# FFN down projection: sixteen of 22 inner tiles as seven block products, sums and splits through PSUM, parts split amid the up projection

## The chip, the core and the metric

The kernel runs on one core of a Trainium2 chip. The metric is the device time of one execution, in microseconds (us). The core has five engines with queues of their own, which meet only at semaphores: TensorE (PE in the profile, PEld its weight loads), VectorE (DVE), ScalarE (ACT), GpSimd (POOL) and SyncE (SP), whose queue issues the DMA transfers. Operands lie in SBUF, matmul results in PSUM, and the inputs, outputs and scratch arrays in HBM.

## The reference

One decoder layer on 1024 tokens of width 1024. The change lies in its last part, a gated MLP with 2816 = 22 x 128 inner channels:

```
h = rms_norm(x, pre_ffn_norm[l])
u = causal_dwconv(h @ ffn_w_up[l], ffn_conv_w[l], ffn_conv_b[l])
gate, val = jnp.split(u, 2, axis=-1)
f = (jax.nn.gelu(gate, approximate=True) * val) @ ffn_w_down[l]
x = x + rms_norm(f, post_ffn_norm[l])
```

All of it is float32. The kernel works on transposed data: 128 channels on the partitions, 512 tokens (a half, h = 0 or 1) along a row.

## The kernel before, in words

**Products.** A float32 operand is split in two numbers of a shorter format: `hi` is the rounded value (a ScalarE copy), `lo` the rest (a subtraction). A product is three matmuls, hi x hi, hi x lo and lo x hi, summed in a PSUM bank. All matmuls are issued in line 203. The tail's pool `psd` has five banks (`dense`), `psn` three more.

**Up projection.** For inner tiles f = 4 to 21, `up_pair` makes gate and value tile in one go, by seven block products in place of eight (Winograd's form of Strassen's scheme): the weights and the activations are cut in 2 x 2 blocks, four weight sums are made on GpSimd and split (`weights7`), the activations' sums `rhs` were made earlier. Each of the seven products is 12 matmuls. Three banks x, y, z accumulate: x takes products 1, 6, 5 and 3 in turn, y takes 2, z takes 7 and 4. Between two of them ScalarE copies the bank's state to SBUF (`snap`), and what is to be subtracted or added is done by VectorE or GpSimd. A causal convolution (`conv`, lines 301 to 309), the gelu (L1471) and the gating product (L1475) follow, and the gated tile goes to HBM (`m_d`).

**First splits.** In eight of these pairs, `first_split` loads a tile of chunk 0 back, splits it (L1449, L1450) and stores both parts (`mhi_d`, `mlo_d`).

**Down projection.** It runs over chunks of inner tiles, `DOWN`: 4, 4, 4, 4, 2 and at last 4 tiles. For each of eight output tiles j and both halves, `down` makes the products of a chunk in one bank and adds it to the sum `acc[h][j]` (L1584, L1586). `m_split` loads and splits a chunk's tiles, `load_w` (L265 to L268) loads and splits the weights, with GpSimd's subtraction. The last chunk goes in three groups of tokens (`LAST`) with the norm behind each; its weights are split ahead by VectorE (`w_split`). `x1_d`, the residual, comes by two 2 MB transfers.

**Order.** A scheduler places the instructions on each engine's queue by its own estimates; pools with a fixed number of buffers (`hi`, `lo` 16 each, `x` 26, `u0`, `u1` four each) and explicit edges bind it. Each queue then runs strictly in order, so an instruction that waits holds up all behind it on its engine.

Of the kernel before, what the change touches and what calls it, by code (L numbers as in the profile page):

```python
# [1241 lines left out]
def tail_stage(nc, tc, es, env):  # L1242
# [144 lines left out]
    def weights7(src0, src1, n):  # L1387

        raws = []
        for m, src in enumerate((src0, src1)):  # L1390
# [24 lines left out]
        return {1: (whi[:, lo], wlo[:, lo]), 2: (whi[:, up], wlo[:, up]), 3: (h24[:, up], l24[:, up]),  # L1415
                4: (ahi, alo), 5: (h31[:, up], l31[:, up]), 6: (h24[:, lo], l24[:, lo]), 7: (h31[:, lo], l31[:, lo])}

    def product(ps, w, rhs, q, first):
        hi, lo = w[q]
        for k, b in enumerate(rhs[q]):  # L1420
            s = slice(k * 128, (k + 1) * 128)
            for n, (x, y) in enumerate(((hi, b[0]), (hi, b[1]), (lo, b[0]))):
                mm(ps, x[:, s], y, start=first and k == 0 and n == 0, stop=k == len(rhs[q]) - 1 and n == 2,
                   skip_group_check=True)

    def bank():
        return psd.tile([128, 512], F32, name="dense", tag="dense")

    def snap(ps):
        s = up_.tile([128, 512], F32, name="snap", bufs=5)  # L1430
        act(s, ps, AF.Copy)
        return s
# [10 lines left out]

    def first_split(f, h):
        raw = x_t(F32)
        nc.sync.dma_start(raw, m_d[f * 128:(f + 1) * 128, hs(h)])
        yield
        parts = [up_.tile([128, 512], R32, name=f"u{s}") for s in range(2)]
        act(parts[0], raw, AF.Copy)  # L1449
        V.tensor_tensor(parts[1], raw, fl(parts[0]), op=OP.subtract)  # L1450
# [39 lines left out]
    def up_pair(f, rhs, between=None):  # L1490

        st = {}
        w = weights7(A["wup"][2 * f], A["wup"][2 * f + 1], 512)
# [4 lines left out]
        V.tensor_tensor(y, y, s1, op=OP.add)
        conv(2 * f, 0, y, st)
        product(x, w, rhs, 6, False)  # L1500
        s2 = snap(x)
# [8 lines left out]
        V.tensor_tensor(z, z, s2, op=OP.subtract)  # L1510
# [47 lines left out]

    acc = []

    def m_tile(f, h, s):
        t = up_.tile([128, 512], F32, name=f"u{s}")
        nc.sync.dma_start(t, m_d[f * 128:(f + 1) * 128, hs(h)])
        return t

    def m_split(f, h):
        src = m_tile(f, h, f % 2)
        hi, lo = hi_t(), lo_t()
        act(hi, src, AF.Copy)
        V.tensor_tensor(lo, src, fl(hi), op=OP.subtract)  # L1570
        return hi, lo

    def m_chunk(f0, nf):
        return {(f, h): m_split(f, h) for h in range(2) for f in range(f0, f0 + nf)}

    def down(ci, f0, nf, ms, ws=()):
        end = None
        for j in range(8):
            w = ws[j] if j < len(ws) else load_w(A[f"wdn{ci}"][j], nf * 128)
            pss = fm_unit(psd, w, lambda k, h: ms[f0 + k, h], nf)  # L1580
            for h, ps in enumerate(pss):
                a = acc[h][j]
                if ci == 0:
                    act(a, ps, AF.Copy)  # L1584
                else:
                    end = V.tensor_tensor(a, a, ps, op=OP.add)  # L1586
# [18 lines left out]
    tc.keep_in_program_order(nc.scalar.preload_act_table_set(E.TABLE))
    for ci, (f0, nf) in enumerate(DOWN[:last]):
        if ci == 0:
            acc = [[x_t(F32) for _ in range(8)] for _ in range(2)]
        i = down(ci, f0, nf, m_chunk(f0, nf) if ci else ms0, () if ci else ws0)
        if ci == last - 2:  # L1610
            late = i
# [5 lines left out]
    def w_split(j, place):
        ws.append(load_w(A[f"wdn{last}"][j], 512, place, up_.tile([128, 512], F32, name="snap", bufs=5)))

    for k in range(nf):  # L1620
        ms[k][0] = m_split(f0 + k, 0)
    for j in range(4):
        w_split(j, (x_t(), x_t()))
    for k in range(nf):
        ms[k][1] = m_split(f0 + k, 1)
    for j in range(4, 8):
        w_split(j, (hi_t(), lo_t()))
    wx_.close()
    x1p = es.enter_context(tc.tile_pool(name="x1", reuse_waits="tile", bufs=1))
    x1s = [x1p.tile([128, 8, 512], F32, name=f"x1_{h}") for h in range(2)]  # L1630
    with tc.issue_after(late.ins):
        for h in range(2):
# [69 lines left out]
```

## Time and profile before

| | |
|---|---|
| median of 3 runs | 2251.07 us (2251.02 to 2253.52) |
| the profiled execution | 2251.32 us, of which the profile's span is 2249.6 us |
| mean granted TensorE clock | 0.989 |
| DMA traffic over the span | 213.44 MB, mean 95 GB/s |
| up pairs | about 1646 to 1992 us of the span |
| down projection and its norms | from there to the end |

The sums in the prediction are made against the profiled execution, 0.25 us above the median. Busy time of TensorE counts a matmul's whole latency, so its share says only when it is idle, not how fast it goes.

### The profile page before, as it was taken

The page shows a single profiled execution, that of the slowest core. Times are in us where ns is not written, and L with a number is a line of the kernel's source. Part 1 is how long each engine was busy: PE and PEld are TensorE (multiplying, and loading weights), DVE is VectorE, ACT ScalarE, POOL GpSimd, SP SyncE. Part 2 cuts the span into 40 slices and gives each one's busy share as a digit, 9 for nine tenths or more (in the row PEclk, how much of TensorE's full clock was granted, in tenths as well). Part 3 has the DMA queues.
Part 4 walks back from the last instruction along what each step waited for, and adds up shares of the span by engine and source line. Part 5 has one row for each costly group of instructions (what it writes and reads, how often), then busy time and mean ns, then how long its engine had stood idle before and what let it go on. Part 6 is the DMA issues. An engine that isn't in the chain of part 4 may idle for free.

```text
span 2249.6 us, 29858 instructions
## 1 busy us (share of the span) xinstructions
PE 2172.8 (97%) x10793; PEld 1763.4 (78%) x10793; DVE 1305.5 (58%) x2415; ACT 1176.7 (52%) x2141; POOL 1049.9 (47%) x725
## 2 busy tenths in 40 slices
PE   7999999999999999999999999999899999999997
PEld 7997667667887878777777788888778888888886
DVE  8324784771477676858484443338776666634346
ACT  7144676676476677545454322245565565653224
POOL 4112565575333322444343245545488888832213
PEclk9999999999999999999999999999999999999998
DMA  5223112201111111331223363344322332374212
GB/s 199 84 84 104 52 35 77 64 8 49 52 39 56 43 52 42 104 108 62 99 75 120 124 200 119 130 144 157 107 88 79 126 125 93 114 273 130 77 29 75
DMA packets 112195, 213.44 MB, mean 95 GB/s; under 512 B 27760, under 2 KB 41904, under 8 KB 112048
## 3 DMA queue, kind: packets, MB, share of 16 engines
q1 hardware_dynamic: 111760, 211.32, 28.7%
q8 instruction: 85, 1.39, 0.3%
q14 instruction: 62, 0.51, 0.1%
q10 hardware_dynamic: 288, 0.22, 0.0%
HBM read 162.67 MB, written 48.82 MB: 94 GB/s over the span
## 4 chain that ended last, share of the span: by engine, by line
PE 85%; DVE 8%; ACT 3%; issue 2%; DMA 1%; POOL 1%; DVEq 0%; SPq 0%; ACTq 0%; POOLq 0%
PE dense L203 67%; PE ps_s L203 6%; PE ps_o L203 5%; PE ps_t L203 4%; PE ps_b L203 2%; DVE u L309 1%; DVE mx L832 1%; DMA cum<-acum_d 1%; DVE x L1656 0%; DVE x L1534 0%; ACT h_hi L395 0%; ACT wT L856 0%; DVE dec L1154 0%; DVE row L524 0%; DVE row L1219 0%
## 5 line engine op out<-in xcount | busy, mean ns | idle before, releaser
L268 POOL TENSOR_TENSOR wlo<-wraw,whi 128x1024 fp32r<-128x1024 f32 (+2 forms) x158 | 320.7, 2030 | 568.7 <-ACT whi L267 544.0
L203 PE MATMUL dense<-h_hi,whi 128*128 128x512 f32 x992 | 400.8, 404 | 10.0 <-DVE row L524 6.3
L203 PE MATMUL dense<-h_hi,wlo 128*128 128x512 f32 x992 | 389.7, 393 | 0.0
L203 PE MATMUL dense<-h_lo,whi 128*128 128x512 f32 x992 | 389.4, 393 | 0.0
L267 ACT ACTIVATE whi<-wraw 128x1024 fp32r<-128x1024 f32 (+2 forms) x158 | 141.3, 894 | 315.2 <-PE dense L203 270.3
L203 PE MATMUL dense<-hi,whi 128*128 128x512 f32 x688 | 270.6, 394 | 9.4 <-ACT hi L1374 6.1
L203 PE MATMUL dense<-lo,whi 128*128 128x512 f32 x688 | 269.0, 392 | 0.0
L203 PE MATMUL dense<-hi,wlo 128*128 128x512 f32 x688 | 263.1, 392 | 4.8 <-POOL wlo L1399 4.8
L203 PEld LDWEIGHTS dense<-h_hi,whi 128*128 128x128 f32 x992 | 187.9, 189 | 51.3 <-issue 6.6
L203 PEld LDWEIGHTS dense<-h_hi,wlo 128*128 128x128 f32 x992 | 187.0, 189 | 40.7 <-issue 0.8
L203 PEld LDWEIGHTS dense<-h_lo,whi 128*128 128x128 f32 x992 | 187.8, 189 | 35.0 <-issue 0.2
L867 POOL TENSOR_TENSOR wT_lo<-wT,wT_hi 128x512 fp32r<-128x512 f32 x132 | 168.7, 1288 | 87.2 <-ACT wT_hi L866 77.9
L203 PEld LDWEIGHTS dense<-hi,whi 128*128 128x128 f32 x688 | 130.3, 190 | 38.7 <-ACT hi L1374 6.5
L203 PEld LDWEIGHTS dense<-hi,wlo 128*128 128x128 f32 x688 | 130.2, 189 | 32.9 <-POOL wlo L1399 5.2
L203 PEld LDWEIGHTS dense<-lo,whi 128*128 128x128 f32 x688 | 130.0, 189 | 28.0 <-issue 0.7
L1067 POOL TENSOR_TENSOR s_lo<-sa,s_hi 128x512 fp32r<-128x512 f32 (+2 forms) x48 | 53.8, 1124 | 151.2 <-ACT s_hi L1066 148.3
L203 PE MATMUL dense<-x,uhi 128*128 128x512 f32 x360 | 116.7, 389 | 0.0
L856 ACT ACTIVATE wT<-ps_s 128x512 f32<-128x512 f32 x132 | 78.4, 594 | 63.7 <-PE ps_s L203 58.6
L309 DVE SCALAR_TENSOR_TENSOR u<-dense,pv,u 128x510 f32<-128x510 f32 (+1 forms) x140 | 101.4, 741 | 8.6 <-ACT u L305 6.9
L1586 DVE TENSOR_TENSOR x<-x,dense 128x512 f32<-128x512 f32 x64 | 43.8, 686 | 86.7 <-PE dense L203 86.6
L866 ACT ACTIVATE wT_hi<-wT 128x512 fp32r<-128x512 f32 x132 | 82.3, 629 | 16.5 <-POOL wT L858 15.0
L203 PE MATMUL ps_s<-Q,K 128*128 128x512 f32 x264 | 83.6, 398 | 4.2 <-DVE Q L843 4.1
(418 smaller groups left out, 5111.9 us busy)
## 6 DMA issues: line engine op xcount, KB each, us to landing
wraw<-in_wfm SPq DMA_DIRECT2D x62, 512.0 KB, 3.4
wraw<-in_wup SPq DMA_DIRECT2D x52, 512.0 KB, 3.3
g_d<-gate_e SPq DMA_DIRECT2D x48, 256.0 KB, 2.0
ge<-g_d SPq DMA_DIRECT2D x24, 512.0 KB, 3.8
m_d<-u SPq DMA_DIRECT2D x44, 256.0 KB, 2.0
u<-m_d SPq DMA_DIRECT2D x36, 256.0 KB, 4.1
cum<-acum_d SPq DMA_DIRECT2D x32, 256.0 KB, 3.2
wraw<-in_wo SPq DMA_DIRECT2D x16, 512.0 KB, 3.3
```

The source lines that it names most:

```text
L203: i = f(*a, **k)
L267: act(hi, raw, AF.Copy)
L268: (eng or (V if tiles else P)).tensor_tensor(lo, raw, fl(hi), op=OP.subtract)
L309: end = V.scalar_tensor_tensor(o[:, d:], ps[:, :512 - d], taps[d], o[:, d:], op0=OP.mult, op1=OP.add)
L832: V.tensor_reduce(mx[:, h, a, n:n + 1] if i >= 4 else MM[:, h, 96 + a:97 + a], pm[:, :w], axis=AX, op=OP.max)
L856: act(w.rearrange("p h q -> p (h q)"), pz, AF.Exp)
L866: act(hi, wf, AF.Copy)
L867: P.tensor_tensor(lo, wf, fl(hi), op=OP.subtract)
L1067: (P if SB_SLO else V).tensor_tensor(s_lo[:, c0:], a[:, c0:], fl(s_hi[:, c0:]), op=OP.subtract)
L1586: end = V.tensor_tensor(a, a, ps, op=OP.add)
```

## The change

Of the 22 inner tiles, `DOWN` now has chunks of 2, 4, 4, 4, 4 and 4. The first (2) and the last (4) are multiplied as before. The four in the middle go by seven block products: `down_pair` takes two output tiles, both halves and a chunk's four inner tiles as 2 x 2 blocks of two tiles each, so a product is 6 matmuls; its banks go as in `up_pair`, and the seven sums go straight to `acc`. `weights7_down` loads and splits the weights of a pair with ScalarE and GpSimd.

The chunk's rows are made by `down_rows`, a chunk ahead, in steps between the pairs: products 1, 2 and 3 need plain tiles, whose parts were split in the up projection and come from HBM (`parts`); products 6, 7, 5 and 4 need sums, made by VectorE with one operand in PSUM, where ScalarE copies it (`in_psum`), and split likewise (`split_to`). So `first_split` now takes 22 tiles (`early`), one or two in most pairs. In `up_pair` the snapshot of product 7 goes to PSUM, and its subtraction moves from GpSimd (L1508 before) to VectorE. Chunk 0 may start only behind the last product of the up projection (`final`), and the two loads of the residual lie at other places, the first in the buffers of chunk 1's rows.

```diff
-DOWN = [(0, 4), (4, 4), (8, 4), (12, 4), (16, 2), (18, 4)]
+DOWN = [(0, 2), (2, 4), (6, 4), (10, 4), (14, 4), (18, 4)]
...
+    def in_psum(src):
+        p = psn.tile([128, 512], F32, name="psn", tag="psn")
+        act(p, src, AF.Copy)
+        return p
+
+    def split_to(hi, lo, src):
+        p = in_psum(src)
+        act(hi, p, AF.Copy)
+        V.tensor_tensor(lo, p, fl(hi), op=OP.subtract)
+        return hi, lo
...
         parts = [up_.tile([128, 512], R32, name=f"u{s}") for s in range(2)]
-        act(parts[0], raw, AF.Copy)
-        V.tensor_tensor(parts[1], raw, fl(parts[0]), op=OP.subtract)
+        split_to(*parts, raw)
...
+    early = [(f, h) for h in range(2) for f in range(DOWN[0][1])]
+    for f0, _ in DOWN[1:-1]:
+        early += [(f0 + k, 0) for k in range(4)] + [(f0 + k, 1) for k in (2, 3)]
...
         product(z, w, rhs, 7, True)
-        s7 = snap(z)
+        s7 = in_psum(z)
         product(x, w, rhs, 5, False)
         s3 = snap(x)
-        P.tensor_tensor(s7, s7, s3, op=OP.subtract)
+        V.tensor_tensor(s7, s7, s3, op=OP.subtract)
...
+    def weights7_down(src0, src1):
+        n = 256
...
+        act(whi[:, first], raw[:, first], AF.Copy)
+        P.tensor_tensor(wlo[:, first], raw[:, first], fl(whi[:, first]), op=OP.subtract)
+        P.tensor_tensor(u1, a21, a22, op=OP.add)
+        P.tensor_tensor(u2, u1, a11, op=OP.add)
+        P.tensor_tensor(u4, u2, a12, op=OP.add)
+        act(h24, f24, AF.Copy)
+        P.tensor_tensor(l24, f24, fl(h24), op=OP.subtract)
+        P.tensor_tensor(u3, a11, a21, op=OP.add)
+        act(h31, f31, AF.Copy)
+        P.tensor_tensor(l31, f31, fl(h31), op=OP.subtract)
+        act(whi[:, last_], a22, AF.Copy)
+        P.tensor_tensor(wlo[:, last_], a22, fl(whi[:, last_]), op=OP.subtract)
...
+    def down_pair(ci, p, r):
+        w = weights7_down(A[f"wdn{ci}"][2 * p], A[f"wdn{ci}"][2 * p + 1])
+        (c11, c12), (c21, c22) = [[acc[h][2 * p + m] for h in range(2)] for m in range(2)]
+        x, y, z = bank(), bank(), bank()
...
+        product(x, w, r, 1, True)
+        s1 = snap(x)
+        product(y, w, r, 2, True)
+        add(y, s1)
+        add(c11, y)
+        product(x, w, r, 6, False)
+        s2 = snap(x)
+        product(z, w, r, 7, True)
+        add(c22, z)
+        product(x, w, r, 5, False)
+        s3 = in_psum(x)
+        add(c22, s3, OP.subtract)
+        product(z, w, r, 4, False)
+        add(z, s2, OP.subtract)
+        add(c21, z)
+        product(x, w, r, 3, False)
+        return add(c12, x)
+
+    def down_rows(f0, places={}):
+        r = {q: [None] * 2 for q in range(1, 8)}
+        raws = [[m_tile(f0 + k + 2 * b, h, k, places.get((k, b, h))) for b in range(2) for h in range(2)]
+                for k in range(2)]
+        yield r
...
+        b11, b12, b21, b22 = zip(*raws)
+        for q, b in ((1, 0), (2, 2)):
+            for k in range(2):
+                r[q][k] = parts(f0 + b + k, 0, two())
+        yield
+        for k in range(2):
+            p = in_psum(b12[k])
+            V.tensor_tensor(b22[k], p, b22[k], op=OP.subtract)
+            V.tensor_tensor(b12[k], b11[k], p, op=OP.subtract)
+            p = in_psum(b22[k])
+            V.tensor_tensor(p, p, b11[k], op=OP.subtract)
+            r[6][k] = hi, lo = x_t(), x_t()
+            act(hi, p, AF.Copy)
+            V.tensor_tensor(lo, p, fl(hi), op=OP.subtract)
+            V.tensor_tensor(b21[k], p, b21[k], op=OP.add)
+        yield
+        split(7, b22, two)
+        split(5, b12, two)
+        split(4, b21, two)
+        for k in range(2):
+            r[3][k] = parts(f0 + 2 + k, 1, two())
...
+    with tc.issue_after(final[0].ins):
+        for j, _ in enumerate(down(0, DOWN[0][1], ms0, ws0)):
+            if j in (1, 3, 5):
+                next(steps, None)
...
+    for ci in range(1, last):
+        steps, now = down_rows(DOWN[ci + 1][0]) if ci < last - 1 else last_rows(), r
+        for p in range(4):
+            if p == 0:
+                r = next(steps)
+            late = down_pair(ci, p, now)
+            if p > 0:
+                next(steps, None)
```

Three places show how the order moves. First, VectorE's queue in a steady up pair; `dense` is a bank, `snap` and `u0`, `u1` are SBUF tiles, `psn` is PSUM, `pv` the taps. Before:

```order
L309 SCALAR_TENSOR_TENSOR u1_16251<-dense_16159,pv_65,u1_16251 128x511
L309 SCALAR_TENSOR_TENSOR u1_16251<-dense_16159,pv_65,u1_16251 128x510
L309 SCALAR_TENSOR_TENSOR u1_16270<-snap_16220,pv_65,u1_16270 128x511
L1475 TENSOR_TENSOR u0_16188<-u0_16188,u1_16251 128x512
L309 SCALAR_TENSOR_TENSOR u1_16270<-snap_16220,pv_65,u1_16270 128x510
L1450 TENSOR_TENSOR u1_16288<-x_16129,u0_16287 128x512
```

And now:

```order
L309 SCALAR_TENSOR_TENSOR u1_16157<-dense_16065,pv_65,u1_16157 128x511
L309 SCALAR_TENSOR_TENSOR u1_16157<-dense_16065,pv_65,u1_16157 128x510
L309 SCALAR_TENSOR_TENSOR u1_16176<-psn_16126,pv_65,u1_16176 128x511
L1513 TENSOR_TENSOR dense_16240<-dense_16240,snap_16254 128x512
L1490 TENSOR_TENSOR u0_16094<-u0_16094,u1_16157 128x512
L309 SCALAR_TENSOR_TENSOR u1_16176<-psn_16126,pv_65,u1_16176 128x510
L1439 TENSOR_TENSOR u1_16194<-psn_16195,u0_16193 128x512
L1439 TENSOR_TENSOR u1_16202<-psn_16203,u0_16201 128x512
```

The steps of the value tile's second half read `psn` in place of `snap`, and two splits (L1439) stand where one (L1450) stood.

Second, TensorE's queue in the last up pair, where its products 6 and 7 meet; `uhi`, `ulo` are weight sums, `x` row sums, `whi` with `hi_18310` chunk 0. Before:

```order
L203 MATMUL dense_18247<-x_15261,uhi_18235 128x512
L203 MATMUL dense_18247<-x_15260,ulo_18236 128x512
L203 MATMUL dense_18249<-x_15110,uhi_18233 128x512 [waits DVE_49,Activation_49]
L203 MATMUL dense_18249<-x_15111,uhi_18233 128x512
L203 MATMUL dense_18438<-hi_18310,whi_18300 128x512 [waits DMAHW6_49,DVE_49]
L203 MATMUL dense_18438<-lo_18311,whi_18300 128x512 [waits DMAHW5_49]
L203 MATMUL dense_18438<-hi_18310,wlo_18301 128x512
```

And now:

```order
L203 MATMUL dense_18463<-x_15261,uhi_18451 128x512
L203 MATMUL dense_18463<-x_15260,ulo_18452 128x512
L203 MATMUL dense_18465<-x_15110,uhi_18449 128x512 [waits DVE_49,Activation_49]
L203 MATMUL dense_18465<-x_15111,uhi_18449 128x512
L203 MATMUL dense_18465<-x_15110,ulo_18450 128x512 [waits Pool_49]
L203 MATMUL dense_18465<-x_15161,uhi_18449 128x512
L203 MATMUL dense_18465<-x_15162,uhi_18449 128x512
```

Chunk 0's products no longer stand between those of the last up pair.

Third, SP's queue where the rows of the next chunk are loaded; `u0`, `u1` are tiles from `m_d`, `wraw` weights, `hi` and `lo` parts. Before, ahead of chunk 3 (12 to 15):

```order
L1563 DMA u0_19658<-m_d_14791 128x512 [waits DMAHW6_49,DVE_49]
L1563 DMA u1_19664<-m_d_14791 128x512 [waits DVE_49]
L1563 DMA u0_19670<-m_d_14791 128x512 [waits DVE_49]
L1563 DMA u1_19676<-m_d_14791 128x512 [waits DVE_49]
L1563 DMA u0_19858<-m_d_14791 128x512 [waits DVE_49]
```

And now, ahead of chunk 3 (10 to 13):

```order
L1579 DMA u0_19302<-m_d_14791 128x512 [waits DMAHW6_49,Activation_49]
L1598 DMA wraw_19597<-in_wdn2 128x512 [waits DMAHW7_49,Pool_49]
L1598 DMA wraw_19597<-in_wdn2 128x512 [waits DMAHW0_49]
L1579 DMA u1_19310<-m_d_14791 128x512 [waits DMAHW1_49,Activation_49]
L1579 DMA u0_19304<-m_d_14791 128x512 [waits DMAHW2_49,Activation_49]
L1579 DMA u1_19312<-m_d_14791 128x512 [waits DMAHW3_49,Activation_49]
L1468 DMA hi_19290<-mhi_d_14792 128x512 [waits DMAHW4_49,PE_49]
L1468 DMA hi_19294<-mhi_d_14792 128x512 [waits DMAHW5_49,PE_49]
L1468 DMA lo_19291<-mlo_d_14793 128x512 [waits DMAHW6_49]
L1468 DMA lo_19295<-mlo_d_14793 128x512 [waits DMAHW7_49]
```

The loads of chunk 2's last parts (`hi_19290` to `lo_19295`, for its product 3) now stand behind raw loads of the next chunk, which wait until ScalarE has copied the tiles that lay there.

More of the change, by code (lines that the diff above doesn't have):

```diff
@@ L1566, in m_split, with down @@
     def m_split(f, h):
[L1567 to L1577, printed above, removed]
+        return split_to(hi_t(), lo_t(), m_tile(f, h, f % 2))
+    def down(f0, nf, ms, ws):
         for j in range(8):
-            w = ws[j] if j < len(ws) else load_w(A[f"wdn{ci}"][j], nf * 128)
-            pss = fm_unit(psd, w, lambda k, h: ms[f0 + k, h], nf)
+            pss = fm_unit(psd, ws[j], lambda k, h: ms[f0 + k, h], nf)
@@ new lines, in down_rows, with split, two @@
+    def down_rows(f0, places={}):
[3 more added lines that the diff above has]
+        yield r
+        def split(q, ts, place):
+            for k, t in enumerate(ts):
+                r[q][k] = split_to(*place(), t)
+        def two():
+            return hi_t(), lo_t()
+        b11, b12, b21, b22 = zip(*raws)
[13 more added lines that the diff above has]
+            V.tensor_tensor(b21[k], p, b21[k], op=OP.add)
+        yield
+        split(7, b22, two)
[3 more added lines that the diff above has]
+            r[3][k] = parts(f0 + 2 + k, 1, two())
@@ L1601, in tail_stage @@
+    for f in range(N_FIRST, NFF):
+        steps = []
+        while early and len(steps) < 2 and early[0][0] <= f - 2:
+            steps.append(first_split(*early.pop(0)))
+        for x in steps:
+            next(x)
         up_pair(f, rhs, begin_down if f == NFF - 1 else None)
-        next(steps, None)
+        for x in steps:
+            next(x, None)
+    assert not early
     last = len(DOWN) - 1
     tc.keep_in_program_order(nc.scalar.preload_act_table_set(E.TABLE))
[L1606 to L1611, printed above, removed]
+    more_down()
@@ new lines, in tail_stage @@
+    wx_.close()
+    wd_ = ExitStack()
+    x1p = es.enter_context(tc.tile_pool(name="x1", reuse_waits="tile", bufs=1))
+    x1s = [x1p.tile([128, 8, 512], F32, name="x1_0")]
+    wd = wd_.enter_context(tc.tile_pool(name="wd", side="right", reuse_waits="tile", bufs=1))
+    acc = [[x_t(F32) for _ in range(8)] for _ in range(2)]
+    steps = down_rows(DOWN[1][0], {(k, 1, h): x1s[0][:, 2 * k + h, :] for k in range(2) for h in range(2)})
+    r = next(steps)
[3 more added lines that the diff above has]
+                next(steps, None)
@@ L1615, in tail_stage, with w_split, last_rows @@
     ws = []
[L1617 to L1632, printed above, removed]
+    def w_split(j, place, raw):
+        ws.append(load_w(A[f"wdn{last}"][j], 512, place, raw))
+    def last_rows():
+        yield
+        for k in range(nf):
+            ms[k][0] = m_split(f0 + k, 0)
+        yield
+        for j in range(3):
+            w_split(j, (x_t(), x_t()), up_.tile([128, 512], F32, name="snap", bufs=5))
+        yield
+        w_split(3, (x_t(), x_t()), E.wp.tile([128, 512], F32, name="wraw", bufs=2))
+        for k in range(nf):
+            ms[k][1] = m_split(f0 + k, 1)
+        for j in range(4, 8):
+            w_split(j, (hi_t(), lo_t()), up_.tile([128, 512], F32, name="snap", bufs=5))
+    for ci in range(1, last):
+        steps, now = down_rows(DOWN[ci + 1][0]) if ci < last - 1 else last_rows(), r
+        for p in range(4):
+            if p == 0:
+                r = next(steps)
+            late = down_pair(ci, p, now)
+            if p > 0:
+                next(steps, None)
+        if ci == last - 2:
+            middle = late
+    wd_.close()
+    x1q = es.enter_context(tc.tile_pool(name="x1b", side="right", reuse_waits="tile", bufs=1))
+    x1s.append(x1q.tile([128, 8, 512], F32, name="x1_1"))
+    for h, i in enumerate((middle, late)):
+        with tc.issue_after(i.ins):
             nc.sync.dma_start(x1s[h], E.x1_d[:, hs(h)].rearrange("(a p) t -> p a t", p=128))
```

69 lines of the change are left out of this document (46 added, 23 removed).

## The prediction

> **What bounds it now.** I read the page's totals first, then the busy time by stage, then the chain that ended last, then who waits for whom in the stages that the change touches. From the page, the span, TensorE's total and the shares of the chain:
> ```profile
> span 2249.6 us, 29858 instructions
> PE 2172.8 (97%) x10793; PEld 1763.4 (78%) x10793; DVE 1305.5 (58%) x2415; ACT 1176.7 (52%) x2141; POOL 1049.9 (47%) x725
> PE 85%; DVE 8%; ACT 3%; issue 2%; DMA 1%; POOL 1%; DVEq 0%; SPq 0%; ACTq 0%; POOLq 0%
> ```
> TensorE carries the chain. By stage (first row the up pairs, second the down projection, third its busiest stretch for DMA; columns are length, busy us of each engine with instruction counts, clock, DMA share, GB/s):
> ```profile
> 1660.00:1990.00 330.00, 326.68 (x1440) 269.58 (x1439) 208.67 (x246) 200.27 (x352) 264.31 (x151) 1.00 0.33 112
> 1990.00:2213.00 223.00, 223.00 (x1010) 185.70 (x1009) 91.76 (x139) 73.44 (x129) 45.93 (x38) 1.00 0.33 109
> 1990.00:2005.00 15.00, 15.00 (x68) 12.43 (x67) 6.29 (x10) 8.55 (x16) 2.56 (x2) 1.00 0.85 285
> ```
> The down projection never leaves TensorE idle, and the others are nearly free there (VectorE 41%, ScalarE 33%, GpSimd 21%). The up pairs lose 3.3 us of 330 with VectorE at 63%, ScalarE 61%, GpSimd 80%. The chain says the same (start, length, what), and TensorE's timeline gives the step of a 512-column matmul, nine steps between these two:
> ```profile
> 1869.50 343.31 PE dense L203 x1536
> ```
> ```profile
> 2109.89 0.39 PE L203 MATMUL dense<-hi,wlo 128*128 128x512 f32 x1
> ...
> 2111.93 0.39 PE L203 MATMUL dense<-hi,wlo 128*128 128x512 f32 x1
> ```
> (2111.93 - 2109.89)/9 = 0.2267 us; the 0.39 is a latency and overlaps. Matmuls taken from here shorten the end one for one as long as nothing new makes TensorE wait.
>
> **A, matmuls removed.** Sixteen inner tiles cost 16 x 8 output tiles x 2 halves x 3 = 768 matmuls. As sixteen pairs of seven products of 2 x 3 they cost 672. The other six tiles keep theirs. 96 x 0.2267 = **-21.8 us**.
>
> **B, the up pairs.** Both halves of the edit stand here: the block sum leaves GpSimd for a VectorE operation with a PSUM operand, its two convolution steps then read PSUM, and splits go from 8 to 22 (one or two in most pairs), each now through PSUM. Forms in 1660 to 1990 (busy, mean ns, idle before), the wait of TensorE, and the end of the chain into the last of its three waits:
> ```profile
> L309 DVE SCALAR_TENSOR_TENSOR u<-snap,pv,u 128x510 f32<-128x510 f32 x17 | 42.4, 2496 | 0.0
> L309 DVE SCALAR_TENSOR_TENSOR u<-dense,pv,u 128x510 f32<-128x510 f32 x51 | 37.6, 744 | 1.4
> L1450 DVE TENSOR_TENSOR u<-x,u 128x512 fp32r<-128x512 f32 x8 | 14.2, 1777 | 0.0
> L1510 DVE TENSOR_TENSOR dense<-dense,snap 128x512 f32<-128x512 f32 x17 | 11.9, 699 | 88.2 <-PE dense L203 88.0
> L1431 ACT ACTIVATE snap<-dense 128x512 f32<-128x512 f32 x69 | 38.7, 586 | 11.1 <-PE dense L203 11.1
> ```
> ```profile
> PE dense L203 <- DVE u L309: 3.3, 3, 1.1
> ```
> ```profile
> 1864.37 1.77 DVE u L309
> 1866.14 1.70 DVE u L1450
> ```
> The last wait (the other two read alike) ends a chain through just the two VectorE forms with both operands in SBUF, which take two to three times as long as the same work on a PSUM operand. Per pair VectorE loses 2.50 - 0.74 = 1.8 us there and gains 0.70 for the sum and 2 x 0.70 for two splits (before: 1.78 in the eight pairs that had one): about even, but without the long operations. GpSimd is rid of one operation in each pair. ScalarE gets 0.6 us of copy and 0.6 of rounding more for each split, 2.4 us on some 11.5 of a 19.0 us pair, which its idle 39% covers. Fourteen more splits are 42 more 256 KB transfers on SP's queue at 112 GB/s, while 285 GB/s was moved above. Ends: -3.3 us if the waits go, +3.3 if the fuller ScalarE queue makes as many again. The rows stand nearer the first: **-2.0**.
>
> The Trainium skill, "SBUF — State Buffer", Who interferes with whom, says that a VectorE operation with two SBUF inputs contends with a GpSimd operation that reads SBUF, and that one with at most one SBUF input does not. The 2496 against 744 ns agree. By that rule the long rows would shrink to the PSUM row's length, as the term has it; it also says that operations which keep two SBUF inputs gain nothing, and term F has eight of those.
>
> **C, the seam.** Before, chunk 0's products stood between the last up pair's, so its copies were hidden; now chunk 0 may only start behind that pair, and in its 96 matmuls (21.8 us) ScalarE has to do the block sums and splits of chunk 1 too. ScalarE's and the other engines' prices, by form:
> ```profile
> L267 ACT ACTIVATE whi<-wraw 128x512 fp32r<-128x512 f32 x29 | 18.3, 630 | 94.7 <-PE dense L203 84.7 <-issue 9.8
> L267 ACT ACTIVATE whi<-wraw 128x256 fp32r<-128x256 f32 x8 | 3.3, 416 | 18.1 <-PE dense L203 16.3 <-issue 1.8
> L1584 ACT ACTIVATE x<-dense 128x512 f32<-128x512 f32 x15 | 8.8, 589 | 9.9 <-PE dense L203 9.9
> L1605 ACT ACT_TABLE_LOAD x1 | 1.3, 1283 | 0.0
> L1337 ACT ACTIVATE psn<-x 128x512 f32<-128x512 f32 x14 | 8.3, 594 | 6.2 <-DVE x L1365 6.2
> L1586 DVE TENSOR_TENSOR x<-x,dense 128x512 f32<-128x512 f32 x64 | 43.8, 686 | 86.7 <-PE dense L203 86.6
> L268 DVE TENSOR_TENSOR lo<-snap,hi 128x512 fp32r<-128x512 f32 x4 | 2.6, 682 | 0.0
> L268 POOL TENSOR_TENSOR wlo<-wraw,whi 128x512 fp32r<-128x512 f32 x30 | 39.7, 1323 | 126.0 <-ACT whi L267 126.0
> L268 POOL TENSOR_TENSOR wlo<-wraw,whi 128x256 fp32r<-128x256 f32 x8 | 6.3, 783 | 20.2 <-ACT whi L267 20.2
> ```
> Rows of a chunk cost ScalarE 10 copies into PSUM (0.594) and 8 roundings (0.59): 10.6 us. In chunk 0 stand besides 16 evictions (9.4), the table load (1.3) and the weights of a pair and a half (3.5): 24.8 us in 21.8, though what the later products need may come some 6 us later. Ends: 0 if that slack is used in full; +6.3 if the overhang of 3.0 shows and the last pair, alone now, waits three times for 1.1 us as above. I take **+2.5**, under the middle, because the products that come first read parts that come by DMA.
>
> **D, the sixteen pairs.** One pair is 42 x 0.2267 = 9.52 us of TensorE. ScalarE: three 512-wide weight roundings, a 256-wide one, two snapshots and a copy into PSUM, 1.89 + 0.42 + 1.17 + 0.59 = 4.1, plus a quarter of 10.6: 6.7 us (71%). VectorE: seven adds and a quarter of 16 row operations, 11 x 0.69 = 7.6 (80%), all with a PSUM operand. GpSimd: three 512-wide subtractions and five 256-wide operations, 3 x 1.32 + 5 x 0.78 = 7.9 (83%). Nobody exceeds TensorE; GpSimd is as full as in the up pairs, VectorE fuller. An accumulating bank goes through a ScalarE copy three times in a pair; the order puts 14 to 18 other matmuls (3.2 to 4.1 us) between, against a copy of 0.59. Ends: 0; and 0.5 us a pair, half of the wait of 1.1 above in every pair: 8. Nearest are the up pairs, which lost 1% at such loads: 1% of 152 us, **+1.5**.
>
> **E, the turnovers.** At each of the four the last product needs parts (rows 3) whose two loads stand on SP's queue behind loads that wait until ScalarE has copied the last sums, as the order above shows. Landing times (KB, median us) and SP's pace of issue:
> ```profile
> hi<-mhi_d SPq DMA_DIRECT2D x8, 256.0 KB, 5.1
> u<-m_d SPq DMA_DIRECT2D x36, 256.0 KB, 4.1
> x<-x_d SPq DMA_DIRECT2D x2, 2048.0 KB, 12.3
> ```
> ```profile
> 1993.33 0.91 SPq L1563 DMA_DIRECT2D u<-m_d  x2
> ```
> From the last copy to the landing: four issues of 0.45 and 4.1 to 5.1 us, about 6 to 7 us. TensorE has some 20 to 30 matmuls (4.5 to 6.8 us) before it needs them. Ends 0 and 2.5 for each of the later three; at the first, the 2 MB load of the residual stands ahead (12.3) and 62 matmuls (14 us) cover it: 0 to 3. I take 1.0 for each: **+4.0**. Bytes do not bound: some 40 MB in 200 us are 200 GB/s.
>
> **F, the end.** Eight weight splits of the last chunk are subtractions in SBUF on VectorE, now beside GpSimd's work: 0.68 each as in the row above, or 1.78 as L1450. VectorE has 36 x 0.69 + 8 x 0.68 to 1.78 = 30 to 39 us for the last chunk's 38.1. Ends 0 and 3; **+1.0**, since half of them are wanted only later.
>
> **Sum.** The profiled execution took 2251.3 us; the median of the three runs is 0.2 below. 2251.3 - 21.8 - 2.0 + 2.5 + 1.5 + 4.0 + 1.0 = **2236.5 us**.
>
> **Rivals.** (1) All hidden: the helpers keep TensorE as full as in the stage before, and B goes to its low end: 2251.3 - 21.8 - 3.3 = 2226, with small waits up to 2231. For it: not one wait in 223 us before; against it: 71 to 83% load and shorter products. (2) VectorE paces the pairs: it is in order, and each add waits for a ScalarE copy. It has 9.5 - 7.6 = 1.9 us free in a pair; if its waits take 2.9, sixteen pairs grow by 1.0 each and the time is 2236.5 - 1.5 + 16 = 2251, no change; at 2.4 it is 2243. Against it: the copies start far ahead in the order. (3) Slower: the turnovers. If SP's queue makes each wait as long as TensorE's one long wait before the change, the clock goes too:
> ```profile
> 1635.55 0.39 PE L203 MATMUL dense<-lo,whi 128*128 128x512 f32 x1
> 1640.73 0.79 PE L203 MATMUL dense<-hi,wlo 128*128 128x512 f32 x1 [4.80 <-POOL wlo L1399]
> 1641.33 0.63 PE L203 MATMUL dense<-hi,whi 128*128 128x512 f32 x1
> 1641.75 0.63 PE L203 MATMUL dense<-lo,whi 128*128 128x512 f32 x1
> ```
> After 4.80 us idle the step is 0.42 instead of 0.227, for about nine matmuls: 1.8 us on top. Four turnovers at 6.6 are 26.4 instead of 4.0: 2259. It gets slower by over 0.2% from 5.8 us a turnover on. For it: 12.3 us of a load ahead of the first; against it: the other three have only 256 KB loads ahead.
>
> "TensorE: Matmul & The Clock Gate" of the Trainium skill, The HAM clock gate, states that an idle window of about 3.4 us halves the clock until a busy one has passed. Four waits of that length would be 4 x (3.4 + 1.8) = 21 us and give about 2253. The trace agrees with both sides of it: 4.80 us halved the clock, 1.1 us did not.
>
> **Chances.** A measurement of this kernel tells 0.2% (4.5 us) from no change. Forecast (2231 to 2243) 0.55; all hidden 0.20; VectorE paces 0.15, a third of it still faster, the rest same; turnovers 0.10, nearly all slower. Faster 0.80, same 0.11, slower 0.09. The range runs from the first rival's low end to where the second still saves a little: 2227 to 2248.
>
> **What would show it.** A: 96 fewer matmuls at 0.227 us. B: the L309 form with 2496 ns gone, no wait of TensorE on L309. C: TensorE waits on ScalarE in the 30 us round the table load, 2 to 3 us in all. D: VectorE near 80% and idle of TensorE under 0.2 us a pair. E: TensorE waiting for a transfer of `hi` or `lo` once in each chunk. F: a wait on VectorE just ahead of the last group. I am wrong if the pairs themselves lose over 0.5 us each, or if one wait passes 3 us and takes the clock along.

## The result, and the profile after

The changed kernel takes 2235.14 us (median of 4 runs, 2234.44 to 2238.14), the kernel before 2251.95 us on the same chip (2251.02 to 2253.52). The ratio is 0.9925, with a 95% interval from 0.9912 to 0.9937. The profiled execution took 2234.44 us. Medians and ratios here and below are of fast runs: one execution of e3 (4322.70 us) and one of e13 (6846.23 us) were slow and are left out.

From the page of the changed kernel, the span and the engines' totals:

```profile
span 2232.7 us, 30175 instructions
PE 2156.0 (97%) x10697; PEld 1746.2 (78%) x10697; DVE 1356.4 (61%) x2537; ACT 1261.3 (56%) x2316; POOL 1093.5 (49%) x798
```

TensorE has 96 records fewer (10793 before) and the span is 16.9 us shorter, not 21.8. Busy time by stage shows where to look (up pairs; the last up pair and the seam; the sixteen pairs; columns as before):

```profile
1660.00:1970.00 310.00, 310.00 (x1368) 256.42 (x1367) 195.73 (x269) 212.04 (x375) 229.55 (x129) 1.00 0.47 157
1970.00:1990.00 20.00, 18.11 (x79) 14.33 (x79) 14.06 (x21) 14.89 (x31) 10.33 (x9) 1.00 0.79 273
2012.00:2165.00 153.00, 151.17 (x650) 121.61 (x649) 103.99 (x165) 88.87 (x171) 103.25 (x111) 1.00 0.53 179
```

The up pairs no longer leave TensorE idle; the seam and the pairs leave 1.9 and 1.8 us each. The chain that ended last names both places (start, length, what):

```profile
1659.36 313.58 PE dense L203 x1381
1972.94 1.28 POOL alo L1413
...
1975.19 2.36 POOL ulo L1411
1977.59 70.96 PE dense L203 x309
...
2098.00 5.11 DMA lo<-mlo_d
2103.15 32.11 PE dense L203 x137
...
2142.87 53.15 PE dense L203 x253
```

One stretch of 313.58 us has taken the place of the up pairs' stretches with a wait between them. At the seam GpSimd's weight subtraction is waited for; later a transfer of `lo` at a turnover (once more at 2058.48). Who waits for whom on TensorE between 1660 and 2196 (total, times, longest):

```profile
PE dense L203 <- POOL ulo L1411: 1.7, 1, 1.7
PE dense L203 <- DMA lo<-mlo_d: 1.6, 2, 1.1
PE dense L203 <- ACT uhi L1410: 0.2, 1, 0.2
```

That is 3.5 us, and it does not explain 16.9 against 21.8 plus the 3.3 of waits that went. Two things are not in such a list. A matmul's 0.39 us of latency hides the first 0.17 us of every wait, so losses have to be read from start to start. And some matmuls simply step more slowly. TensorE's timeline in the first pair of the down projection, with combined weights, five steps between these rows:

```profile
2012.64 0.40 PE L203 MATMUL dense<-hi,vhi 128*128 128x512 f32 x1
...
2013.81 0.40 PE L203 MATMUL dense<-hi,vlo 128*128 128x512 f32 x1
```

(2013.81 - 2012.64)/5 = 0.234 us, against the 0.2267 of before. Over the stage 2012 to 2165, leaving out steps over 0.29 us, the mean is 0.2328 us for 357 matmuls with `vhi` or `vlo` and 0.2282 for 271 with `whi` or `wlo`; in the up pairs it is 0.2267. The 0.2282 comes mostly from the borders between the two: thirty steps from a `whi` or `wlo` matmul to one with `vhi` or `vlo` take 0.2331 us on the mean, 211 between two of their own kind 0.2272.

Start to start, the account of the spans is:

| place | us |
|---|---|
| 96 matmuls x 0.2267 | -21.8 |
| up pairs: before, three steps of 1.50, 1.51 and 1.49 us and a slow one of 0.31 behind each; now none | -4.1 |
| seam: steps of 0.58, 2.43 (for two) and 0.34 us | +2.4 |
| turnovers near 2062, 2102 and 2142: 1.4, 1.0 and 0.9 us | +3.3 |
| slower steps: 384 x 0.0061 + 288 x 0.0015 | +2.8 |
| stage begins 0.7 later (a weight transfer landed later), tail 0.1 longer | +0.8 |
| sum, against 2232.7 - 2249.6 = -16.9 | -16.6 |

### The profile page after: what moved, and what is told of

It is laid out like the page before. It is cut to its first block, busy times and chain, and to the rows that moved or that the text cites. A ratio compares the mean times of both kernels' runs of the same rounds, so it can differ in the third digit from the quotient of the medians.

```text
span 2232.7 us, 30175 instructions
## 1 busy us (share of the span) xinstructions
PE 2156.0 (97%) x10697; PEld 1746.2 (78%) x10697; DVE 1356.4 (61%) x2537; ACT 1261.3 (56%) x2316; POOL 1093.5 (49%) x798
## 4 chain that ended last, share of the span: by engine, by line
PE 85%; DVE 7%; ACT 4%; issue 2%; DMA 1%; POOL 1%; SPq 0%; DVEq 0%; ACTq 0%; POOLq 0%
PE dense L203 67%; PE ps_s L203 6%; PE ps_o L203 6%; PE ps_t L203 5%; PE ps_b L203 2%; DMA lo<-mlo_d 1%; DVE mx L832 1%; DVE dec L1154 1%; DVE x L1796 0%; DVE x L1549 0%; ACT h_hi L395 0%; DVE row L524 0%; ACT wT L856 0%; DVE row L1219 0%; POOL wT_lo L867 0%
## 5 line engine op out<-in xcount | busy, mean ns | idle before, releaser
L268 POOL TENSOR_TENSOR wlo<-wraw,whi 128x1024 fp32r<-128x1024 f32 (+1 forms) x118 | 271.5, 2303 | 421.4 <-ACT whi L267 396.8
L267 ACT ACTIVATE whi<-wraw 128x1024 fp32r<-128x1024 f32 (+1 forms) x118 | 117.8, 999 | 196.6 <-PE dense L203 178.0
L203 PE MATMUL dense<-hi,whi 128*128 128x512 f32 x512 | 201.9, 396 | 6.1 <-ACT hi L1374 6.1
L203 PE MATMUL dense<-hi,wlo 128*128 128x512 f32 x512 | 199.6, 393 | 5.5 <-POOL wlo L1399 5.5
L203 PE MATMUL dense<-lo,whi 128*128 128x512 f32 x512 | 200.4, 393 | 0.0
L203 PEld LDWEIGHTS dense<-hi,whi 128*128 128x128 f32 x512 | 97.3, 190 | 27.5 <-ACT hi L1374 6.5
L203 PEld LDWEIGHTS dense<-hi,wlo 128*128 128x128 f32 x512 | 96.9, 189 | 26.7 <-POOL wlo L1399 5.9
L203 PEld LDWEIGHTS dense<-lo,whi 128*128 128x128 f32 x512 | 96.9, 189 | 21.6 <-issue 0.7
L309 DVE SCALAR_TENSOR_TENSOR u<-dense,pv,u 128x510 f32<-128x510 f32 (+1 forms) x140 | 101.6, 741 | 9.1 <-ACT u L305 7.9
L203 PEld LDWEIGHTS dense<-x,uhi 128*128 128x128 f32 x360 | 67.4, 188 | 14.8 <-ACT uhi L1410 0.9
```

The costliest lines, as they stand in the source:

```text
L203: i = f(*a, **k)
L267: act(hi, raw, AF.Copy)
L268: (eng or (V if tiles else P)).tensor_tensor(lo, raw, fl(hi), op=OP.subtract)
L309: end = V.scalar_tensor_tensor(o[:, d:], ps[:, :512 - d], taps[d], o[:, d:], op0=OP.mult, op1=OP.add)
```

## Experiments

All ratios are to the kernel before, timed on the same chip as the run; the changed kernel's is 0.9925 [0.9912, 0.9937]. The runs come from several chips, on which the kernel before took 2251.95 to 2253.11 us, so ratios compare better than medians. Effects of 2 to 3 us lie within two such intervals, so for a single one the trace decides, not the time.

| run | median us | ratio, 95% interval |
|---|---|---|
| e1_sum_in_sbuf | 2242.57 | 0.9954 [0.9941, 0.9966] |
| e2_split_in_sbuf | 2234.71 | 0.9918 [0.9905, 0.9932] |
| e9_sum_in_sbuf_seam | 2234.48 | 0.9921 [0.9909, 0.9933] |
| e3_seam_order | 2232.03 | 0.9908 [0.9893, 0.9923] |
| e4_parts_first | 2231.98 | 0.9908 [0.9894, 0.9922] |
| e5_sides | 2231.59 | 0.9905 [0.9892, 0.9919] |
| e11_gap_128 | 2233.07 | 0.9911 [0.9897, 0.9924] |
| e12_gap_384 | 2234.79, one run | none |
| e6_vector_more | 2235.30 | 0.9921 [0.9908, 0.9935] |
| e7_rows_in_sbuf | 2238.21 | 0.9935 [0.9923, 0.9948] |
| e10_all | 2227.07 | 0.9886 [0.9873, 0.9900] |
| e13_all_y | 2225.28 | 0.9879 [0.9864, 0.9894] |

### Which half of the up-pair edit took the waits away

**e1_sum_in_sbuf.**

```diff
-        s7 = in_psum(z)
+        s7 = snap(z)
...
-        V.tensor_tensor(s7, s7, s3, op=OP.subtract)
+        P.tensor_tensor(s7, s7, s3, op=OP.subtract)
```

> The changed kernel with one half of the up-pair edit undone: the block sum is again copied to SBUF and subtracted there by GpSimd; the splits keep their copy into PSUM. Theory S (the sum alone held TensorE back): the 510-wide L309 form of about 2.5 us is back 17 times, TensorE waits on L309 about three times for 1.1 to 1.3 us as before the change, and the time is about 3.8 us above the changed kernel, 2239. Theory P (the split with SBUF operands, 1.7 us, was the part that made the wait long): the 2.5 us form is back but TensorE does not wait, and the time is that of the changed kernel, 2235. Theory both (each needs the other, since the chain into the wait was one of each): as theory P here.

It lost 6.5 us by the ratios, but not where any theory had it. The first two rows are its VectorE form with SBUF operands and the stretch 1660 to 1970, then TensorE's longest waits, then its timeline behind them:

```profile
L309 DVE SCALAR_TENSOR_TENSOR u<-snap,pv,u 128x510 f32<-128x510 f32 x16 | 35.6, 2225 | 0.0
1660.00:1970.00 310.00, 309.00 (x1361) 254.94 (x1360) 199.89 (x251) 213.91 (x379) 259.56 (x146) 1.00 0.44 153
```

```profile
PE dense L203 <- POOL ulo L1411: 2.0, 1, 2.0
PE dense L203 <- ACT uhi L1410: 1.5, 1, 1.5
```

```profile
1986.87 0.63 PE L203 MATMUL dense<-hi,uhi 128*128 128x512 f32 x1
1987.29 0.63 PE L203 MATMUL dense<-x,uhi 128*128 128x512 f32 x1
```

The long form is back, and none of the waits of 1.1 us for L309 is. Of the 1.0 us that TensorE is idle in this stretch, 0.78 is a wait for a snapshot; L309 still ends two waits of 0.11 us, at 1792.52 and 1926.17, which cost 0.35 us each from start to start. But GpSimd, 260 us busy of 310 instead of 230, comes to the last pair later: 1.55 and 2.02 us of waiting at the seam, and from 1982.4 to 1988.6 a step of 0.42 us, half clock.

**e2_split_in_sbuf**, the other half undone:

```diff
-        split_to(*parts, raw)
+        hi, lo = parts
+        act(hi, raw, AF.Copy)
+        V.tensor_tensor(lo, raw, fl(hi), op=OP.subtract)
```

> The changed kernel with the other half undone: the splits amid the up projection subtract from the SBUF tile, without the copy into PSUM; the block sum stays in PSUM on VectorE. The 22 splits of two subtractions each grow from 0.68 to about 1.75 us on VectorE. Theory P (the split made the wait): TensorE waits on L309 come back, at least three of 1.1 us and more since most pairs now have two splits, 4 us or more above the changed kernel. Theory S and theory both: no wait, time as the changed kernel, 2235.

```profile
L1464 DVE TENSOR_TENSOR u<-x,u 128x512 fp32r<-128x512 f32 x27 | 38.1, 1444 | 1.1 <-ACT u L1463 1.1
```

The splits take 1.44 us each (0.676 in the changed kernel) and no wait on L309 appears; the time is the changed kernel's. Theories S and P each predicted about three waits of 1.1 us or more from one half alone and fall. Of the three, "both" is left for the waits on L309: with either half of the edit in place they are gone, but for the 0.7 us in e1. No run has both halves undone, so that this edit took them away, and not another part of the change, is argued and not shown. That the sum also costs time elsewhere none of the theories had, so it got a run of its own.

**e9_sum_in_sbuf_seam** is e1 with the order of e3 below.

> The block sum back on GpSimd in SBUF, as in the first run, together with the order at the seam of the third run. The first run lost 7 us against the changed kernel, with no wait of TensorE on L309: 4.0 us at the seam instead of 2.1, and behind it steps of 0.425 us for some 6 us. Theory G (the sum's price is paid at the seam alone, where GpSimd is late with the last pair's weights): the waits on uhi and ulo shrink to 1 us or less, the long steps go, and the time falls to 2234 to 2236. Rival H (GpSimd, 84% busy in the up pairs, is late there whatever stands ahead): the waits on ulo stay over 1.5 us and the time over 2239.

```profile
PE dense L203 <- POOL ulo L1411: 0.5, 1, 0.5
```

The wait on `uhi` and the half clock are gone, and some 7.4 us with them by the ratios (0.9954 to 0.9921). Theory G holds: what GpSimd's extra operation cost was paid at the seam, but for the same two short waits on L309 in the pairs (0.7 us).

### The seam

**e3_seam_order.** In `more_down`; `ends` holds the last rounding to `uhi` (L1410) and the last subtraction to `ulo` (L1411) of the pair's weights.

```diff
-            act(hi, r, AF.Copy)
-            P.tensor_tensor(lo, r, fl(hi), op=OP.subtract)
+            with tc.issue_after(ends[0].ins):
+                act(hi, r, AF.Copy)
+            with tc.issue_after(ends[1].ins):
+                P.tensor_tensor(lo, r, fl(hi), op=OP.subtract)
```

> The changed kernel in which the rounding of chunk 0's later weights stands behind the last up pair's last weight rounding on ScalarE, and its subtraction behind the pair's last weight subtraction on GpSimd; nothing else moves. Theory W (at the seam ScalarE, in order, stood 4.8 us waiting for the transfer of those weights, and the pair's weights came late behind it): TensorE's waits on ulo (1.7 us) and uhi (0.2) go, 2.1 us less, 2233. Theory L of the prediction (ScalarE has more work than time at the seam): the wait only moves, to a copy of chunk 0 or to the first products of chunk 1, and the time stays at 2235.

The rows of the changed kernel behind it are these (ScalarE's and GpSimd's timelines):

```profile
1970.97 0.63 ACT L1705 ACTIVATE x<-wraw 128x512 fp32r<-128x512 f32 x1 [4.82 <-DMA wraw<-in_wdn]
...
1974.06 1.04 ACT L1410 ACTIVATE uhi<-uf 128x1024 fp32r<-128x1024 f32 x1
```

```profile
1975.18 2.35 POOL L1411 TENSOR_TENSOR ulo<-uf,uhi 128x1024 fp32r<-128x1024 f32 x1 [0.96 <-ACT uhi L1410]
```

ScalarE stood 4.82 us for the transfer of chunk 0's later weights, and the last pair's own weights waited behind it. With the two swapped, all of TensorE's waits between 1660 and 2196 are:

```profile
PE dense L203 <- DMA lo<-mlo_d: 1.8, 2, 0.9
PE dense L203 <- DMA hi<-mhi_d: 0.5, 1, 0.5
```

The seam's losses fell from 2.4 to 0.6 us and did not move to a copy of chunk 0: theory W, against the prediction's own reason L. The turnovers, now reached earlier, took a part back (3.3 to 3.9 us).

### The turnovers

**e4_parts_first.** In `down_rows`; `parted[1]` is the last load of the rows-3 parts, `rows()` makes the eight raw loads (`m_tile`).

```diff
+            with tc.issue_after(parted[1].ins):
+                raws = rows()
```

> The changed kernel in which the loads of the raw rows stand on SP's queue behind the loads of the rows-3 parts, for the parts of chunks 2 and 3; for those of chunk 4 the order is as it was. Theory Q (the parts come late because they stand behind raw loads that wait for ScalarE): TensorE's losses near 2062 (1.5 us) and 2102 (1.0 us) go, that near 2142 (0.9 us) stays, 2.4 us less, 2233. Rival R (the raw rows, now later, make the block sums late): new waits on x, hi or lo from VectorE or ScalarE in the second or third pair of a chunk, 1 us or more each, and a time of 2236 to 2240. Rival D (the transfer itself is slow, 5 us whenever it is issued, and buffers come free no earlier): nothing changes.

SP's queue near the second turnover, in the changed kernel and then in this run:

```profile
2095.15 2.32 SPq L1579 DMA_DIRECT2D u<-m_d  x2
2097.57 0.38 SPq L1468 DMA_DIRECT2D hi<-mhi_d  x1
2098.00 0.42 SPq L1468 DMA_DIRECT2D lo<-mlo_d  x1
```

```profile
2092.02 0.84 SPq L1470 DMA_DIRECT2D hi<-mhi_d  x2
2092.91 0.90 SPq L1470 DMA_DIRECT2D lo<-mlo_d  x2
2093.91 5.08 SPq L1581 DMA_DIRECT2D u<-m_d  x8
```

The parts leave 5 us earlier. The losses near 2062 and 2102 are gone, the one in the turnover left as it was (2139 here, 1.0 us) stays, and no wait on the raw rows came up. Theory Q.

### The slower steps

**e5_sides** exchanges two areas of equal size:

```diff
-    x1p = es.enter_context(tc.tile_pool(name="x1", reuse_waits="tile", bufs=1))
+    x1p = es.enter_context(tc.tile_pool(name="x1", side="right", reuse_waits="tile", bufs=1))
...
-    wd = wd_.enter_context(tc.tile_pool(name="wd", side="right", reuse_waits="tile", bufs=1))
+    wd = wd_.enter_context(tc.tile_pool(name="wd", reuse_waits="tile", bufs=1))
...
-    x1q = es.enter_context(tc.tile_pool(name="x1b", side="right", reuse_waits="tile", bufs=1))
+    x1q = es.enter_context(tc.tile_pool(name="x1b", reuse_waits="tile", bufs=1))
```

> The changed kernel with two equal areas of SBUF exchanged: the tiles of the pairs' combined weights (vf, vhi, vlo) stand where the residual stood, and the residual where they stood; every engine's order is the same. In the changed kernel's pairs the step of a matmul whose weights are vhi or vlo is 0.2325 us on the mean, of one with whi or wlo 0.228, against 0.2267 in the up pairs. Theory A (the place of the weights in SBUF sets that step): vhi and vlo fall to about 0.227 and the time by some 2 us, 2233. Theory N (it is not the place, but what the pairs do around it): the steps stay at 0.2325 and the time at 2235.

**e11_gap_128** and **e12_gap_384** leave `wd` where it was but for a gap of 32 or 96 floats (e11 is shown):

```diff
     fw = es.enter_context(tc.tile_pool(name="ffn", side="right", reuse_waits="tile", bufs=1))
+    fw.tile([128, 32], F32, name="gap")
```

> The changed kernel with an unused gap of 128 bytes a partition ahead of the area of vf, vhi and vlo; nothing else moves and every engine's order is the same. In the built programs the start addresses of hi, lo, x, whi, wlo, uhi, ulo in a partition are all 352 modulo 512, those of vhi and vlo in the changed kernel 480, and in the run with exchanged areas 352 again. Theory M (a matmul steps slower where weights and moving operand differ modulo 512, 256 or so): with the gap they agree, the steps of vhi and vlo fall to 0.227 us, and the time falls as with the exchange, by some 2.7 us, to 2232. Theory A2 (it is the area): they stay at 0.2325, 2235.

> The same with a gap of 384 bytes: vhi and vlo stand at 96 modulo 512, 256 from the moving operands. One look, for the steps in its profile. Theory M256 (what counts is the address modulo 256): 0.227 us. Theory M512 (modulo 512): 0.2325. A value between would say that the distance counts.

The same five steps as above, in e5, e11 and e12 (first and last row of each):

```profile
2012.76 0.39 PE L203 MATMUL dense<-hi,vhi 128*128 128x512 f32 x1
...
2013.89 0.39 PE L203 MATMUL dense<-hi,vlo 128*128 128x512 f32 x1
```

```profile
2014.04 0.39 PE L203 MATMUL dense<-hi,vhi 128*128 128x512 f32 x1
...
2015.17 0.39 PE L203 MATMUL dense<-hi,vlo 128*128 128x512 f32 x1
```

```profile
2014.62 0.39 PE L203 MATMUL dense<-hi,vhi 128*128 128x512 f32 x1
...
2015.75 0.39 PE L203 MATMUL dense<-hi,vlo 128*128 128x512 f32 x1
```

1.13/5 = 0.226 us in all three. The stage's means are 0.2268, 0.2268 and 0.2269 us for `vhi` and `vlo`, and 0.2268 for `whi` and `wlo` in each. So neither the area nor the work around it decides, but the address: weights 128 bytes off the moving operand modulo 256 step 2.7% slower, and agreeing modulo 256 is enough (M256). In time the gap alone gave little, since its turnovers lost 5.6 us instead of 3.3: a faster chunk comes sooner to parts that are late.

### The rivals in which VectorE decides

**e6_vector_more** and **e7_rows_in_sbuf**:

```diff
         add(c11, y)
+        for _ in range(3):
+            V.tensor_tensor(spare, c11, y, op=OP.add)
```

```diff
-                r[q][k] = split_to(*place(), t)
+                r[q][k] = hi, lo = place()
+                act(hi, t, AF.Copy)
+                V.tensor_tensor(lo, t, fl(hi), op=OP.subtract)
```

> The changed kernel with three more additions on VectorE in each of the sixteen pairs, each with one operand in PSUM, of which the result goes unused: some 2 us for each pair, the 1.9 us that the prediction counted as free. The scheduler also moves some products of neighbouring pairs against each other. Theory V (VectorE is near pacing the pairs, the prediction's second rival): TensorE waits on VectorE in most pairs and the time grows by 8 to 16 us, to 2243 to 2251. Theory F (VectorE has slack, because its operations follow each other every 0.60 us and not every 0.69): at most two or three waits, under 3 us in all, 2235 to 2238.

> The changed kernel in which the splits of rows 7, 5 and 4 in the down projection subtract in SBUF, without the copy into PSUM, six in a chunk: ScalarE is rid of 3.6 us a chunk, VectorE's subtractions grow from 0.685 to about 1.75 us beside GpSimd's work, 6.4 us a chunk. Theory K (the copy buys VectorE time that TensorE waits for): new waits on lo in the turnovers, 1 us or more each, 2238 to 2245. Theory F (VectorE has the room here, 27 of 39 us used): 2233 to 2236, and the raw rows, let go sooner, may even shorten the losses at the turnovers.

Of e6 the sixteen pairs, and of the changed kernel two rows of VectorE's timeline that follow each other:

```profile
2012.00:2165.00 153.00, 150.36 (x643) 119.96 (x642) 128.99 (x209) 90.86 (x173) 103.51 (x111) 1.00 0.52 177
```

```profile
2089.73 0.68 DVE L1676 TENSOR_TENSOR x<-psn,x 128x512 fp32r<-128x512 f32 x1
2090.33 0.68 DVE L1677 TENSOR_TENSOR u<-psn,u 128x512 f32<-128x512 f32 x1
```

VectorE is busy 129 us of 153 instead of 104, and the list of TensorE's waits names it nowhere. From start to start it held TensorE up twice, in steps of 0.53 us near 2095 and 2136 that an addition (L1629) ended, 0.8 us in all: theory F. The mean of 0.68 counts a tail of 0.08 us that the next operation overlaps. In e7 the splits have the longer form (1.06 us on the mean where 1.75 was expected), and TensorE's waits between 1660 and 2196 change their kind:

```profile
L1660 DVE TENSOR_TENSOR lo<-u,hi 128x512 fp32r<-128x512 f32 x18 | 18.6, 1059 | 0.0
```

```profile
PE dense L203 <- DVE x L1678: 3.2, 2, 1.6
...
PE dense L203 <- DVE x L1629: 1.5, 1, 1.5
PE dense L203 <- ACT hi L1659: 1.1, 2, 0.6
```

VectorE's share hardly moves (107 us of 153), the waits for transfers are gone, and 5.8 us of waiting for sums and splits have come. Theory K has the direction and the size, not the place: it named `lo` at the turnover, and the waits are on the parts of row 6 (`x`), on a sum and on a `hi`. The time rose by 2 to 3 us (0.9935 against 0.9925), within the intervals. The products were also placed in another order, so how much is the longer form's alone stays open.

### A version that beats both

**e10_all** is e3, e4 (with the last chunk's raw rows behind chunk 4's parts too) and the gap of 128 bytes; **e13_all_y** adds the same gap ahead of `yhi` and `ylo`:

```diff
+            br.enter_context(tc.tile_pool(name="ygap", side="right", reuse_waits="tile", bufs=1)).tile([128, 32], F32, name="gap")
             yq = br.enter_context(tc.tile_pool(name="yq", side="right", reuse_waits="tile", bufs=6))
```

> The changed kernel with the order at the seam, the loads of the rows-3 parts ahead of the raw rows for all three later chunks (in the last one ahead of the last group's raw rows), and the gap of 128 bytes. If the three losses add up: 2.1 for the seam, 3.3 for the turnovers, 2.7 for the steps, 8 us below the changed kernel, 2227, and TensorE has no wait over 0.3 us from the up pairs to the last group. If GpSimd or SP only hands a wait on, one of 1 us or more appears elsewhere, and the time is 2229 to 2232.

> As the run before, with a second gap of 128 bytes ahead of the tiles yhi and ylo, which stand at 480 modulo 512 against weights at 352 in 288 matmuls of an earlier stage that the change does not touch; their step in the changed kernel is 0.233 us. If the rule of the addresses holds there too, the steps fall to 0.227 and the time by another 1.8 us, to 2225. If it was something of the pairs, nothing changes.

Of e10 the pairs and the chain's last long piece:

```profile
2008.00:2165.00 157.00, 157.00 (x695) 129.99 (x694) 108.76 (x172) 96.04 (x185) 103.09 (x111) 1.00 0.54 188
1975.04 212.59 PE dense L203 x958
```

From the seam to the tail no wait of TensorE is left, though the seam still loses 0.6 us from start to start; the three losses add up (2227.07 where 2227 was expected). For e13, nine steps of the earlier stage, in the changed kernel and in e13:

```profile
1400.02 0.39 PE L203 MATMUL dense<-ylo,whi 128*128 128x512 f32 x1
...
1402.11 0.40 PE L203 MATMUL dense<-ylo,whi 128*128 128x512 f32 x1
```

```profile
1399.94 0.39 PE L203 MATMUL dense<-yhi,wlo 128*128 128x512 f32 x1
...
1401.98 0.39 PE L203 MATMUL dense<-yhi,wlo 128*128 128x512 f32 x1
```

2.09/9 = 0.232 becomes 2.04/9 = 0.227 us: the rule held in a place for which it was not made. The median fell by 1.8 us more, which two intervals that overlap cannot confirm.

## Why the prediction was right, step by step

**A** (-21.8): 96 records fewer, and steps where nothing interferes of 0.2267. Right.

**B** (-2.0, ends -3.3 and +3.3): -4.1, below the low end. The waits on L309 went as said: the 2.5 us form is gone, its steps read PSUM, and VectorE's work in the stage is as it was (63% of the time). Its rows between 1660 and 1970:

```profile
L1490 DVE TENSOR_TENSOR u<-u,u 128x512 f32<-128x512 f32 x32 | 57.3, 1791 | 5.0 <-ACT u L1486 4.6
...
L309 DVE SCALAR_TENSOR_TENSOR u<-psn,pv,u 128x510 f32<-128x510 f32 x16 | 11.8, 737 | 0.0
...
L1439 DVE TENSOR_TENSOR u<-psn,u 128x512 fp32r<-128x512 f32 x27 | 17.4, 676 | 1.1 <-ACT u L1438 1.1
```

But "without the long operations" failed: the gating product (L1490), with both operands in SBUF, went from 1416 ns (L1475 before) to 1791, fourteen of the 32 take over 2.5 us, and TensorE does not wait for them. Nor do two SBUF operands alone make an operation long. Before the change, the 511-wide step of L309 with the same operands as the 510-wide one took this:

```profile
L309 DVE SCALAR_TENSOR_TENSOR u<-snap,pv,u 128x511 f32<-128x511 f32 x16 | 12.1, 754 | 0.0
```

Fifteen of these sixteen began while GpSimd was idle and took 0.74 us. The sixteen 510-wide ones in the same stretch all began while a GpSimd operation was running and took 1.71 to 2.90 us. (2496 against 744 ns is also 3.4 times, not two to three.)

The size was off because the waits' 1.1 us were taken for their price. A wait of 1.11 is a step of 1.50 in place of 0.227, with one of 0.31 behind it: 1.36. The fear of a fuller ScalarE queue (+3.3) had no counterpart: 212 us busy of 310, and no wait.

The rule cited there from the Trainium skill, "SBUF — State Buffer", Who interferes with whom, on VectorE operations with two SBUF inputs beside GpSimd, agrees with e2: 1444 against 676 ns for the same split.

**C** (+2.5): +2.4, the right size for a wrong reason. The prediction added up ScalarE's work; ScalarE had the time, but it stood still, in order, behind a transfer that was in no sum (e3), and of the 1.9 us of waits 1.7 ended on GpSimd. The failed step is the assumption that what is hoisted into the last pair waits for nothing.

**D** (+1.5): no idle time outside the turnovers, so the helpers' loads, the ground of the term, cost nothing; instead 2.8 us in steps that the prediction held constant at 0.2267. "Idle under 0.2 us a pair" was right and would not have found them. VectorE's predicted 80% was 68% (104 of 153), ScalarE's 71% was 58%, GpSimd's 83% was 67%.

**E** (+4.0): +3.3. The order on SP's queue, the 5.1 us of a landing, and the larger cover of the first turnover were as read; the raw loads ahead waited for ScalarE as said (e4).

**F** (+1.0): 0. TensorE runs 53.15 us without a stop from 2142.87, and the last group follows without a wait ahead of it.

**The sum.** The errors are -2.1 in B, -0.1 in C, +1.3 in D, -0.7 in E and -1.0 in F, and +0.8 of late start and tail: -1.8 together, and the account leaves 0.3. Without their signs the errors of the five terms add up to 5.2 us, so that the total came so close is in part luck.

**The rivals.** "All hidden" was not what the change did, but what it could do: e10 stands at 2227. VectorE does not pace the pairs, even with three more additions in each (e6). The turnovers' waits of at most 1.1 us stayed far from the 5.8 from which they would have decided.

## What to carry to other kernels

Read losses of a busy TensorE from start to start: its list of waits showed 3.5 us here, the steps showed 8.5. An engine that works in order is not described by its load; ask which instruction at its head waits for a transfer, and put urgent work ahead of work that was only hoisted. Where weights and moving operands share a matmul, give their tiles the same address modulo 256 bytes: an area that lay 128 bytes off cost 2.8 us here.

## What the runs showed of the hardware

The step of a float32 matmul of 512 columns depends on where its weights and its moving operand lie: 0.2328 us at 128 bytes apart modulo 256, 0.2267 to 0.2269 when they agree, at 256 bytes' distance too (e5, e11, e12; 0.232 against 0.227 in another stage, e13). Other distances were not tried, nor both operands moved by 128 bytes alike, so whether the distance counts or the one place that was slow in both stages stays open. The Trainium skill, "SBUF — State Buffer", Who interferes with whom, gives TensorE two independent read ports, for the moving operand and for the weights, and says that it never waits for anyone; the slower steps do not fit that, and no run here shows what they wait for.

The clock halved amid waits of 1.55 and 2.02 us with two matmuls between them (e1), while a single one of 1.9 us (e2, at a turnover) left it alone. In e13's profile a single longer one halved it too, in the first up pair, where the step was 0.42 us from 1654.4 to 1657.4:

```profile
1653.00 0.50 PE L203 MATMUL dense<-lo,ahi 128*128 128x512 f32 x1 [2.46 <-ACT psn L1434]
```

The prediction had this effect from one wait of 4.80 us. "TensorE: Matmul & The Clock Gate" of the Trainium skill, The HAM clock gate, speaks of an idle window of about 3.4 us; e1's two waits add up to 3.6, but the 2.46 lies below it. Length alone does not decide. TensorE waits 2.72 or 2.73 us near 804 in every profile here: in the kernel before the granted clock was then 0.50 from 805.5 to 808.5, in the changed kernel it stayed at 1.00, and of the fourteen profiles seven show the one and seven the other. So a wait of 2.5 us, or shorter ones close together, can already take the clock along here, and need not.
